# Where a load stands in the queue: moving token-major loads, rotary tables and four low parts in the preparation of a two-layer encoder

## The chip, the cores and the metric

The kernel runs on one core of a Trainium2 chip. Its engines each work off their own instruction queue in order: TensorE (PE in the profile), VectorE (DVE), ScalarE (ACT), GpSimd (POOL) and SyncE (SP), which issues nearly all transfers here. The metric is the device time of one execution in microseconds (us); lower is better. Lines are written L138 for line 138 of the kernel before; in the changed kernel the lines behind the preparation are numbered three higher (L1033 becomes L1036).

## The reference

A trunk of two layers over 1024 tokens of width 1024, with 256 memory tokens beside it. Cut to what matters here:

```python
memn = rmsnorm(mem, mem_norm_gain)
for l in range(2):
    h = rmsnorm(x, norm_gain[l])
    mk, mv = jnp.split(memn @ w_mem_kv[l], 2, axis=-1)       # memory keys and values, both layers
    if l == 0:
        qa, ka, va, qb, kb, vb, qm, gate = split_cols(h @ w_in_even[0], SPLIT_EVEN)
        qa = rope_2d(rmsnorm(qa, q_norm_a), row, col)         # 8 query heads of 64
        ka = rope_2d(rmsnorm(ka, k_norm_a), row, col)         # 2 key heads of 64
        ya = global_gqa(qa, ka, va)                           # full attention
        yb = window_gqa(qb, kb, vb, sink, rel_bias)
        ym = memory_attn(qm, mk, mv)
        x = x + (concatenate([ya, yb, ym]) * silu(gate)) @ w_out_even[0]
    else:
        ...                                                   # neighbourhood attention in place of A and B
return rmsnorm(x, final_norm_gain)
```

`rope_2d` rotates pairs of a head's elements by angles of the token's grid row and column, with cosine and sine tables. Everything is float32.

## The kernel before, in words

To keep float32 accuracy on TensorE, each operand of a matmul is split into two parts: a high part (a copy in a rounded type, `wh`, `ah`, `H`) and a low part (the value less its high part, `wl`, `al`). Each product is three matmuls: high by high, high by low, low by high.

Layer 0 cannot start before its preparation, `project_a`. In program order that is:

- the tokens' and the memory's columns are loaded (L943) and scaled by the gains; group 0 of the A weights (`a_weights`) gives keys and values for four quarters of 256 tokens (`a_unit`, L851);
- `mem_keys` for layer 0: eight units of weights of 128x512 (two per head); each unit is a load (`wload`, L138), a high part on ScalarE (`wparts`, L125), a low part (L160), and twelve matmuls (L561);
- `mem_values` for layer 0: eight more units, with matmuls at L590; its low parts alternate between VectorE and GpSimd;
- `rope_tables`: gains, cosines and sines are loaded (L764, L768), and GpSimd multiplies them to four tables (L771);
- `rstd(io["mt"], ...)`: the memory's tokens again, token by row this time (token-major, four loads of 128x512, L801), squared and summed on ScalarE (L802), for the factors `rs_m` by which memory rows are normalised after the projection;
- group 1 of the A weights, the same statistics for the tokens (`stats`), key units (`k_unit`), layer 1's memory keys;
- eight query units (`q_unit`), four with group 1 and four with group 2: each takes a projection, normalises and rotates it on ScalarE, VectorE and GpSimd (the sum `rp`, L885), transposes it on TensorE (L133), splits it into a high and a low `so` buffer (L125, L129), and stores the parts with eight DMAs (group 1, L928 and L929) or four (group 2, L931);
- `mem_values` for layer 1 behind the second unit of group 2, all of its low parts on VectorE; and at last `mem_q`, the memory queries of layer 0 (L242), from `w_e` weights.

The raw weights have four buffers, `wraw`; a load into one waits until the high and the low part that read it are made. The order on each engine is not that of the program text alone: the framework's scheduler simulates a timeline (`schedule_with_timeline_sim`) and sorts instructions by it, subject to priorities and to fences. A fence is written as `tc.issue_after(x)`: what is issued inside it does not come before `x` in the order. The lines that bear on the change:

```python
def behind(self):                                             # L120
    return self.tc.issue_after(self.loaded.ins) if self.loaded else nullcontext()
...
self.raws.append(d)                                           # L139, wload: every raw weight load in turn
...
e = self.either() if self.wsplit[1] == "both" else nc.gpsimd if self.wsplit[1] == "pool" else nc.vector
e.tensor_tensor(lf, raw, hf, op=OP.subtract)                  # L160, wparts: the low part
...
with self.behind():                                           # L800, rstd: a token-major load
    nc.sync.dma_start(t, src[b][:, j * 512:j * 512 + 512])
```

`raws[0]` to `raws[3]` are group 0 of the A weights, `raws[4]` to `raws[11]` the eight units of layer 0's memory keys. So `raws[6]` is their third unit, `raws[8]` the fifth and `raws[11]` the eighth. `either()` returns VectorE and GpSimd in turn. In front of `rope_tables` the fence `self.loaded` is the last load of the memory's columns.

## Time and profile before

| what | value |
|---|---|
| time, median of three runs | 1488.08 us (1487.84 to 1490.82) |
| profiled execution: span on the core (the page gives no other time of it) | 1486.8 us |
| median less span | 1.28 us |
| TensorE busy | 1467.6 us, 99% of the span |
| VectorE, ScalarE, GpSimd busy | 69%, 56%, 43% |
| preparation: from the start to the first scores matmul of layer 0 (L1033) | 143.63 us |
| TensorE idle from 20 to 70 us, and from 100 to 125 us | 2.74 us, 1.42 us |

Times inside the profile count from the start of the span. A row of the timeline has the start, the length, engine, line, operation, output and inputs, and in brackets how long the engine was idle before it and what ended that. A row with x4 joins four neighbours of a kind. Rows of a stretch have, after its bounds and length, the busy time and count of PE, PE's weight loads, DVE, ACT and POOL, then the granted TensorE clock, the transfers' share and GB/s. SPq marks rows of SP's queue: the issue of a transfer, not its duration.

### The profile page before, as it was taken

What the parts mean: (1) busy time and instruction counts of PE and PEld (TensorE: products, weight loads), DVE (VectorE), ACT (ScalarE), POOL (GpSimd) and SP (SyncE); (2) the same over time, 40 slices, a digit from 0 to 9 for tenths busy, and PEclk for the clock granted to TensorE, in tenths of its full rate; (3) what the DMA queues carried; (4) which work ended last, traced back from release to release, by engine and by line L of the source; (5) the groups of instructions that cost most, each with busy time, mean ns of one, the idle gap of its engine ahead of it and who ended that gap; (6) DMA issues with size and microseconds to landing.
All of it is one profiled execution on the core that took longest, in us unless ns stands there. A gap on an engine that the chain in (4) does not pass through costs nothing.

```text
span 1486.8 us, 25511 instructions
## 1 busy us (share of the span) xinstructions
PE 1467.6 (99%) x8433; PEld 1274.7 (86%) x8433; DVE 1030.7 (69%) x2124; ACT 837.2 (56%) x1877; POOL 644.2 (43%) x767
## 2 busy tenths in 40 slices
PE   9999999999999999999999999999999999999998
PEld 8898898988888788888879987888998898888886
DVE  6687777677776577776687776664446787778674
ACT  7743665556655456654544444444446777777454
POOL 1223668556765746543450000001425556665454
PEclk9999999999999999999999999999999999999999
DMA  8966334434443424388553343567665568789834
GB/s 287 306 160 181 118 125 160 123 120 133 126 137 112 155 78 144 100 276 303 187 176 127 128 135 137 157 169 241 233 242 170 188 198 269 246 283 323 314 105 144
DMA packets 173860, 271.92 MB, mean 183 GB/s; under 512 B 15648, under 2 KB 96800, under 8 KB 172704
## 3 DMA queue, kind: packets, MB, share of 16 engines
q1 hardware_dynamic: 173296, 270.20, 56.4%
q8 instruction: 67, 1.10, 0.3%
q14 instruction: 65, 0.53, 0.1%
q10 hardware_dynamic: 432, 0.09, 0.0%
HBM read 174.28 MB, written 83.89 MB: 174 GB/s over the span
## 4 chain that ended last, share of the span: by engine, by line
PE 86%; DMA 6%; DVE 3%; ACT 2%; issue 1%; SPq 1%; POOL 1%; POOLq 0%; ACTq 0%; DVEq 0%
PE pj L242 16%; PE pj L62 11%; PE x L1617 6%; PE tr L133 6%; PE pv L1066 4%; PE y L1617 4%; PE pv L62 3%; PE s L62 3%; PE pj L1332 3%; PE tr L62 3%; PE sa L1332 2%; PE pv L1617 2%; PE sa L1033 2%; PE s L1332 2%; PE sa L1034 2%; PE pj L851 2%
## 5 line engine op out<-in xcount | busy, mean ns | idle before, releaser
L542 DVE TENSOR_TENSOR pl<-tr,ph 128x512 fp32r<-128x512 f32 (+2 forms) x352 | 203.9, 594 | 45.5 <-ACT ph L125 43.6
L125 ACT ACTIVATE ph<-tr 128x512 fp32r<-128x512 f32 (+2 forms) x352 | 176.2, 522 | 103.7 <-PE tr L133 79.7
L242 PE MATMUL pj<-H,wh 128*128 128x512 f32 x704 | 233.2, 411 | 0.6 <-DVE vt L313 0.2
L158 POOL TENSOR_SCALAR wh<-wraw 128x512 fp32r<-128x512 f32 x48 | 32.2, 673 | 275.2 <-PE x L1617 236.0
L125 ACT ACTIVATE wh<-wraw 128x384 fp32r<-128x384 f32 (+1 forms) x163 | 88.7, 553 | 99.6 <-PE pj L1332 12.2
L242 PE MATMUL pj<-H,wl 128*128 128x512 f32 x352 | 139.2, 395 | 0.0
L242 PEld LDWEIGHTS pj<-H,wh 128*128 128x128 f32 x704 | 120.6, 189 | 19.3 <-issue 0.6
L62 PE MATMUL pj<-H,wh 128*128 128x512 f32 x384 | 121.0, 396 | 0.0
L1119 POOL TENSOR_SCALAR pn<-pn,st 128x384 f32<-128x384 f32 (+1 forms) x128 | 72.7, 569 | 102.1 <-DVE st L1118 62.0
L133 PE MATMUL tr<-ident,P 128*128 128x128 f32 x752 | 115.4, 273 | 0.3 <-POOL P L719 0.2
L1279 POOL TENSOR_TENSOR wl<-wraw,wh 128x384 fp32r<-128x384 f32 x56 | 62.9, 1125 | 91.5 <-ACT wh L125 89.2
L1117 ACT ACTIVATE pn<-pn,st 128x384 f32<-128x384 f32 (+1 forms) x128 | 75.1, 587 | 41.8 <-DVE st L1114 40.5
L133 PEld LDWEIGHTS tr<-ident,P 128*128 128x128 f32 x752 | 88.9, 140 | 8.2 <-POOL P L719 1.2
L1039 ACT ACTIVATE P<-sa,st 128x1024 f32<-128x1024 f32 x64 | 71.4, 1117 | 35.3 <-PE tr L133 19.1
L1041 POOL TENSOR_SCALAR P<-P,st 128x1024 f32<-128x1024 f32 x64 | 74.6, 1169 | 27.9 <-DVE st L1040 27.3
L1038 DVE TENSOR_REDUCE st<-sa 128x1 f32<-128x1024 f32 x64 | 77.5, 1218 | 8.3 <-PE sa L1034 7.6
L62 PE MATMUL s<-k,q 128*128 128x384 f32 (+1 forms) x352 | 81.2, 327 | 0.0
L242 PEld LDWEIGHTS pj<-H,wl 128*128 128x128 f32 x352 | 66.2, 188 | 15.1
L62 PE MATMUL pj<-H,wl 128*128 128x512 f32 x192 | 75.6, 394 | 0.0
L160 POOL TENSOR_TENSOR wl<-wraw,wh 128x512 fp32r<-128x512 f32 x52 | 69.6, 1341 | 10.3 <-ACT wh L125 7.8
L851 PE MATMUL pj<-ah,H 128*128 128x256 f32 x384 | 70.8, 282 | 1.0 <-ACT ah L125 0.6
L62 PEld LDWEIGHTS pj<-H,wh 128*128 128x128 f32 x384 | 66.6, 188 | 5.4
(568 smaller groups left out, 4186.7 us busy)
## 6 DMA issues: line engine op xcount, KB each, us to landing
wraw<-w_o SPq DMA_DIRECT2D x52, 256.0 KB, 3.7
y<-yb SPq DMA_DIRECT2D x24, 512.0 KB, 3.4
wraw<-s SPq DMA_DIRECT2D x64, 192.0 KB, 3.9
wraw<-w_e SPq DMA_DIRECT2D x44, 256.0 KB, 3.3
k<-k SPq DMA_DIRECT2D x42, 256.0 KB, 5.9
s<-bias SPq DMA_DIRECT2D x56, 192.0 KB, 2.0
wq<-w_o SPq DMA_DIRECT2D x40, 256.0 KB, 3.3
y<-sg SPq DMA_DIRECT2D x18, 512.0 KB, 3.5
```

Of the source, the lines that this page charges most:

```text
L62: return lambda *a, **k: self.tc.keep_in_program_order(getattr(self.engine, name)(*a, **k))
L125: return self.nc.scalar.activation(out, in_, AF.Copy, scale=scale)
L133: self.turned = self.fence = self.pe.transpose(o, i, self.ident)
L242: self.pe.matmul(a[:, :n], s[:, kt % UNIT, :], m, start=(kt == 0 and i == 0), stop=(kt == KT - 1 and i == 2))
L542: self.low = nc.vector.tensor_tensor(pl[:, :n], tr[:, :n], ph[:, :n], op=OP.subtract)
L851: self.last = nc.tensor.matmul(a[:, b * 256:(b + 1) * 256], x[kt][:, t], w, start=(kt + b + i == 0), stop=(kt == KT - 1 and i == 2), skip_ ...
L1038: nc.vector.tensor_reduce(st[:, 0:1], s, axis=AX.X, op=OP.max, negate=True)
L1041: self.normal = nc.gpsimd.tensor_scalar(pt, pt, st[:, 2:3], 0.5, op0=OP.mult, op1=OP.mult)
L1117: nc.scalar.activation(o, o, AF.Exp, bias=st[:, 0:1], scale=-1.0, accum_out=st[:, 2:3])
L1119: self.normal = normal = nc.gpsimd.tensor_scalar(o, o, st[:, 3:4], 0.5, op0=OP.mult, op1=OP.mult)
L1332: last = nc.tensor.matmul(bank, s[:, k, :], y[3 * u + k][m][:, cols], start=start and u + k + e == 0, stop=u == 1 and k + e == 4, skip_gro ...
L1617: self.last = nc.tensor.matmul(bank, ws[s][:, k, :], b[k][m], start=start and k + i == 0, stop=k == UNIT - 1 and i == 2, skip_group_check= ...
```

## The change

Two edits in `project_a`. First, the memory's token-major loads now come ahead of `rope_tables` in the program, behind a fence on the fifth unit of the memory's key weights (before: the third); the three loads of the rotary tables get the eighth unit as their fence (before: the memory's columns). This fence also holds for the loads of A weights and token statistics that follow in the text, which had the third unit's. Second, the eight low parts of layer 1's memory values alternate between VectorE and GpSimd; before all eight were on VectorE. Eight turns of `either()` leave its state as it was.

```diff
@@ -985,10 +985,11 @@
         end = [self.mem_keys(w0, mem, kvd[0], ("pj", "tr"), "so", "rt1")]
         self.wsplit = ("act", "both")
         end.append(self.mem_values(w0, mem, kvd[0], "so"))
+        vm = self.st("xv", [128, 2])
+        self.loaded = self.raws[8]
+        self.rstd(io["mt"], [0, 1], vm, self.rs_m)
+        self.loaded = self.raws[11]
         self.rope_tables()
-        vm = self.st("xv", [128, 2])
-        self.loaded = self.raws[6]
-        self.rstd(io["mt"], [0, 1], vm, self.rs_m)
         self.wsplit = ("act", "dve")
         w1 = self.a_weights(1)
         self.stats(range(4))
@@ -1009,7 +1010,9 @@
         for q in range(4):
             after(self.q_unit(self.a_unit(w2, q), q, 2, qa, qd))
             if q == 1:
+                self.wsplit = ("act", "both")
                 self.mem_values(w1m, mem, kvd[1], "so")()
+                self.wsplit = ("act", "dve")
         while late:
             flush()
         return self.mem_q(io["w_e"], E_QM)
```

The scheduler makes a new order of the preparation from it, on every engine. Behind the preparation the orders agree. Three places matter. SP's queue after the fourth unit of the memory's keys (`wraw_600` is the fifth unit, `wraw_654` the eighth, `xt<-mt` the memory's token-major loads), before:

```order
L138 DMA wraw_581<-w_mem 128x512
L764 DMA so_770<-g_kq 128x256
L768 DMA rt_135_772<-c_cos 128x512
L768 DMA rqn_778<-c_sin 128x512
L801 DMA xt_786<-mt 128x512
L801 DMA xt_789<-mt 128x512
L801 DMA xt_792<-mt 128x512
L138 DMA wraw_600<-w_mem 128x512
L138 DMA wraw_618<-w_mem 128x512
L138 DMA wraw_636<-w_mem 128x512
L801 DMA xt_795<-mt 128x512
L138 DMA wraw_654<-w_mem 128x512
```

and now:

```order
L138 DMA wraw_581<-w_mem 128x512
L138 DMA wraw_600<-w_mem 128x512
L801 DMA xt_772<-mt 128x512
L138 DMA wraw_618<-w_mem 128x512
L138 DMA wraw_636<-w_mem 128x512
L801 DMA xt_775<-mt 128x512
L138 DMA wraw_654<-w_mem 128x512
L801 DMA xt_778<-mt 128x512
L801 DMA xt_781<-mt 128x512
L764 DMA so_792<-g_kq 128x256
L768 DMA rt_142_794<-c_cos 128x512
L768 DMA rqn_800<-c_sin 128x512
```

The fifth unit moved ahead of six transfers, and the tables behind all units. The second place is SP's queue at the end of the preparation. The difference around the stores of the query units; `wraw_1824` and `wraw_1836` are the last two units of layer 1's memory values, `wraw_2039` and `wraw_2045` the two units of layer 0's memory queries, and `so_1529` stands for the third unit's high part:

```order
+L138 DMA wraw_1800<-w_mem 128x4x128
 L912 DMA k_138<-k_138 64x1024
-L138 DMA wraw_1800<-w_mem 128x4x128
 L138 DMA wraw_1812<-w_mem 128x4x128
+L138 DMA wraw_1824<-w_mem 128x4x128
 L928 DMA q_143<-so_1357 64x256
 L929 DMA qa<-so_1357 64x256
```

and, sixteen stores on:

```order
 L929 DMA qa<-so_1444 64x256
-L138 DMA wraw_1824<-w_mem 128x4x128
-L138 DMA wraw_1836<-w_mem 128x4x128
-L138 DMA wraw_2039<-w_e 128x512
-L138 DMA wraw_2045<-w_e 128x512
 L928 DMA q_143<-so_1529 64x256
 L929 DMA qa<-so_1529 64x256
```

and, sixteen more and the first unit of group 2 on:

```order
 L931 DMA qa<-so_1737 64x2x256
 L931 DMA qa<-so_1738 64x2x256
-L599 DMA kv_108<-so_1848 128x4x128
-L599 DMA kv_108<-so_1849 128x4x128
+L138 DMA wraw_1836<-w_mem 128x4x128
+L138 DMA wraw_2039<-w_e 128x512
+L138 DMA wraw_2045<-w_e 128x512
 L138 DMA wraw_2137<-w_e 128x512
```

One of the four loads that stood between the second and the third query unit's stores moved ahead of all of them, and three behind all 36. The third place is TensorE where these three are used, now (`pj_1942` is the last query unit's projection, `pj_1750` and `pj_1751` the memory values, `pj_2051` and `pj_2078` the memory queries):

```order
L851 MATMUL pj_1942<-ah_1566,H_133 128x256
L590 MATMUL pj_1750<-wh_1838,q_142 128x512
L590 MATMUL pj_1751<-wh_1838,q_142 128x512
L133 MATMUL tr_2013<-ident_63,rp_1927 128x128 x4
L242 MATMUL pj_2051<-H_118,wh_2041 128x512
L242 MATMUL pj_2051<-H_126,wh_2041 128x512
L242 MATMUL pj_2078<-H_118,wh_2041 128x512
L242 MATMUL pj_2078<-H_126,wh_2041 128x512
L590 MATMUL pj_1750<-wl_1839,q_142 128x512
L590 MATMUL pj_1750<-wh_1838,mem_177 128x512
L590 MATMUL pj_1751<-wl_1839,q_142 128x512
L590 MATMUL pj_1751<-wh_1838,mem_177 128x512
```

Before, `pj_2051<-H_118,wh_2041` came straight after the last row of `pj_1942`, and the L590 rows of `wh_1838` stood some ninety rows earlier.

## The prediction

> **What bounds the kernel now.** I read the page's busy shares first, then TensorE's waits in the preparation (everything before layer 0's first attention scores), then its stretches, and last the timeline of SP, whose queue turns out to set the end of the changed preparation.
>
> ```profile
> PE 1467.6 (99%) x8433; PEld 1274.7 (86%) x8433; DVE 1030.7 (69%) x2124; ACT 837.2 (56%) x1877; POOL 644.2 (43%) x767
> ```
>
> TensorE is busy 99% of the span and runs in order, so time can be won only where it pauses. Its waits from 0 to 110 us, and from 110 to 144 (line, what it waited for, total, times, longest):
>
> ```profile
> PE tr L133 <- POOL rp L885: 0.8, 1, 0.8
> PE tr L561 <- ACT wh L125: 0.6, 2, 0.4
> PE pj L851 <- ACT ah L125: 0.6, 1, 0.6
> PE tr L561 <- DVE wl L160: 0.5, 2, 0.2
> ...
> PE pj L590 <- ACT wh L125: 0.2, 1, 0.2
> ```
> ```profile
> PE pj L590 <- DVE wl L160: 1.3, 3, 0.8
> ```
>
> The stretches of the preparation (first column of sums PE, third DVE; then clock, DMA share, GB/s):
>
> ```profile
> 20.00:70.00 50.00, 47.26 (x339) 43.31 (x338) 29.80 (x77) 38.08 (x95) 14.59 (x12) 1.00 0.97 306
> ...
> 100.00:125.00 25.00, 23.58 (x149) 20.12 (x148) 23.01 (x53) 10.02 (x22) 5.52 (x4) 1.00 0.61 153
> 125.00:145.00 20.00, 20.00 (x121) 17.57 (x120) 11.64 (x27) 5.65 (x11) 6.00 (x6) 1.00 0.72 197
> ```
> ```profile
> 34.00:39.00 5.00, 3.90 (x26) 3.08 (x25) 2.03 (x7) 3.00 (x9) 1.29 (x2) 1.00 0.92 315
> ...
> 59.00:62.00 3.00, 1.58 (x12) 1.18 (x11) 1.80 (x5) 1.84 (x6) 1.55 (x2) 1.00 1.03 391
> ```
>
> From 20 to 70 us the transfers are the limit (DMA 0.97), from 100 to 125 VectorE is (23.01 of 25 us, TensorE 23.58), and from 125 on TensorE is full. Three pauses of before are open to the early part of the change: 1.10 us at the memory keys (5.00 less 3.90), 0.2 at L590, 1.42 at 59 to 62.
>
> **The change part by part.** *Early loads.* TensorE's pause rows, and what stood behind them:
>
> ```profile
> 35.48 0.38 PE L561 MATMUL tr<-q,wh 128*128 128x256 f32 x1 [0.37 <-ACT wh L125]
> ...
> 61.39 0.62 PE L851 MATMUL pj<-ah,H 128*128 128x256 f32 x3 [0.59 <-ACT ah L125]
> ```
> ```profile
> 34.80 0.63 ACT L125 ACTIVATE wh<-wraw 128x512 fp32r<-128x512 f32 x1 [0.78 <-DMA wraw<-w_mem]
> ```
> ```profile
> 22.81 0.43 SPq L764 DMA_DIRECT2D so<-g_kq  x1
> ...
> 24.63 2.28 SPq L801 DMA_DIRECT2D xt<-mt  x3
> 27.02 2.75 SPq L138 DMA_DIRECT2D wraw<-w_mem  x3
> ```
>
> The fifth key unit was issued at 27.02 behind six other transfers; now it is SP's next row and they follow, mixed with the later units. Its buffer comes free only with VectorE's first low parts:
>
> ```profile
> 26.30 1.96 DVE L160 TENSOR_TENSOR wl<-wraw,wh 128x512 fp32r<-128x512 f32 x3
> ```
>
> So SP now stands from 22.8 to about 27 with nothing issued, but from 27 on the key units find a shorter queue. Seven transfers are moved behind them: six of 256 KB and one of 128, 1.66 MB, 5.4 us at the 306 GB/s of the row above. The key pauses need 2 us, so I take them as gone; at worst (the dry 4 us come back later) nothing is won. The 0.8 us wait for the rotated keys (L133) goes because that transpose now stands 42 rows later, with 42 x 0.12 = 5 us more matmuls ahead of it (three matmuls end 0.62 after the first starts, one 0.38: 0.12 apart). A row's end is modelled, so each pause is 0.26 (0.38 less 0.12) longer between starts than as idle time: 1.10 + 0.2 + 1.42 = 2.7 idle, seven pauses, 2.7 + 1.8 = **4.5 us of lead** for TensorE at 62 us; bounds 0 and 4.5.
>
> The moved tables and statistics cost nothing as far as cover goes: the rotary tables are first read here,
>
> ```profile
> 58.32 0.42 DVE L880 TENSOR_TENSOR rt<-rqn,c_cosk 128x256 f32<-128x256 f32 x1
> ```
>
> and in the changed order they are issued by 35.4 (eleven rows behind 27.02, at the 0.76 of the three at 24.63), 23 us ahead of that read. The memory's row factors are read by VectorE's scaling of the projected keys, and no TensorE wait above names them. Were that cover gone, the projections' PSUM buffers would come free later and the lead would shrink by as much.
>
> *Low parts on GpSimd.* Four of eight L160 subtractions leave VectorE (0.69 us each) for GpSimd:
>
> ```profile
> L160 POOL TENSOR_TENSOR wl<-wraw,wh 128x512 fp32r<-128x512 f32 x52 | 69.6, 1341 | 10.3 <-ACT wh L125 7.8
> ```
> ```profile
> 110.76 1.28 POOL L885 TENSOR_TENSOR rp<-rt,rt 128x512 f32<-128x512 f32 x1 [2.31 <-DVE rt L882]
> ```
> ```profile
> 111.11 1.48 DVE L160 TENSOR_TENSOR wl<-wraw,wh 128x512 fp32r<-128x512 f32 x1
> 112.59 0.68 DVE L160 TENSOR_TENSOR wl<-wraw,wh 128x512 fp32r<-128x512 f32 x1
> ```
>
> GpSimd's take 1.34 us. Beside a GpSimd sum the same VectorE subtraction took 1.48 us, the next one, alone, 0.68: each GpSimd operation can hold VectorE by up to 0.8. The trace has no moved split, so its price on VectorE lies between -0.69 (nothing held) and +0.1.
>
> [...]
>
> *What decides the end: the units' stores.* Of the four moved splits three stood ahead of `so_1530`, while `wl_1827` now stands ahead of it instead of behind: two fewer, 1.4 us. Three GpSimd splits may hold VectorE by 2.4. With the lead, `so_1530` is written 4.5 + 1.4 - 2.4 = **3.5 us earlier**; bounds -1.0 (no lead, full hold) and 5.9 (all lead, no hold). I take the full hold, as VectorE's share (23.01 of 25) leaves hardly a gap in which to run beside GpSimd. This matters because of SP:
>
> ```profile
> 100.88 0.51 SPq L928 DMA_DIRECT2D q<-so  x1
> ...
> 111.62 1.17 SPq L138 DMA_DIRECT2D wraw<-w_mem  x2
> 112.89 0.92 SPq L138 DMA_DIRECT2D wraw<-w_e  x2
> 115.26 0.47 SPq L928 DMA_DIRECT2D q<-so  x1
> ...
> 126.68 2.65 SPq L931 DMA_DIRECT2D qa<-so  x4
> ```
> ```profile
> 115.26 0.69 DVE L129 TENSOR_TENSOR so<-tr,so 128x512 fp32r<-128x512 f32 x1
> ```
>
> Before, the last memory unit and the two units for layer 0's memory queries (`wraw_1836`, `wraw_2039`, `wraw_2045`) were issued at 112 to 113.8, between the second and third unit's stores. In the changed order they stand behind all 36 stores. Before, `so_1530` was written at 115.95 and the last store issued at 129.33, 13.4 later. Sixteen stores alone took 10.7 (100.88 to 111.62, 0.67 each), so fourteen and the last four need at least 9.4 + 2.65 = 12.0. I take 13.4, since the VectorE work between is the same: 115.95 - 3.5 + 13.4 = **125.8** for SP to reach the three loads (124.4 by the other end). How long they take:
>
> ```profile
> wraw<-w_mem SPq DMA_DIRECT2D x2, 256.0 KB, 3.3
> wraw<-w_e SPq DMA_DIRECT2D x2, 256.0 KB, 4.1
> ```
>
> The first `w_e` unit follows 0.6 after, lands 4.1 later and is copied in the 0.63 of ACT's row above: `wh_2041` at **131.1** (0.8 less, if it lands like `w_mem`). TensorE, 4.5 us early, would want it at about 127: a **new pause of 4 us**, released by ACT's copy behind a DMA. What follows it:
>
> ```profile
> 131.60 0.63 PE L242 MATMUL pj<-H,wh 128*128 128x512 f32 x2
> 132.07 0.39 PE L242 MATMUL pj<-H,wl 128*128 128x512 f32 x1
> ...
> 138.10 0.60 PE L133 MATMUL tr<-ident,rp 128*128 128x128 f32 x4
> 138.46 0.48 PE L242 MATMUL pj<-H,wh 128*128 128x512 f32 x1
> ...
> 143.63 0.40 PE L1033 MATMUL sa<-k,q 128*128 128x512 f32 x1
> ```
>
> Before, 12.0 us lay from the first L242 to layer 0. Now four L590 matmuls have moved behind it (4 x 0.235 = 0.9) and one group of four transposes ahead (0.4): 12.5. Layer 0 begins at 131.1 + 12.5 = **143.6**, against 143.63. From there the order on every engine is the old one. The span stays 1486.8, the median lies 1.3 above it (1488.08): **1488.1 us**. The lead is won early and given back at the stores.
>
> **The rivals.**
>
> *A, the lead is kept.* GpSimd's splits fall beside VectorE's short operations, `so_1530` comes 5 us earlier (110.95), SP needs 12.0 behind it, the load lands in 3.3: `wh_2041` at 110.95 + 12.0 + 0.6 + 3.3 + 0.63 = 127.5, layer 0 at 140.0, **1484.4**. For it: SP's pace of 0.67 and the free 0.68 rows; against it: the 1.48 row and VectorE's 23.01.
>
> *B, slower.* The place is SP's row of `wraw_1836`, the price one us per us that SP reaches it after 125.8, and it loses from there on. If VectorE writes `so_1530` no earlier than before, SP is through at 129.35, `wh_2041` is there at 134.7, layer 0 begins at 147.2: +3.6, **1491.7**. For it: VectorE is nearly full from 100 to 125, so a lead of TensorE need not reach it. Against: two subtractions less ahead of it.
>
> *C, the early pauses stay* (the change doesn't do what it says), since the 4 us in which SP issues nothing at 23 to 27 are lost in a stretch where DMA is 0.97 busy. Then `so_1530` gains only 1.4 less a hold of 0.8, 0.6: +3.0 by the same chain, **1491.1**.
>
> *D, the clock falls in the new pause.* The granted clock (third figure from the end) at the kernel's end, where TensorE has little to do:
>
> ```profile
> 1478.00:1480.00 2.00, 0.75 (x8) 0.66 (x6) 1.70 (x5) 0.99 (x4) 1.07 (x1) 1.00 0.04 14
> 1480.00:1482.00 2.00, 0.62 (x4) 0.41 (x4) 1.71 (x5) 0.38 (x1) 1.42 (x3) 0.72 1.08 382
> ```
> ```profile
> 1.31 4.21 PE L970 MATMUL pj<-rp 128*128 128x512 f32 x9 [1.31 <-POOL rp L966]
> ```
>
> It falls after some 3 us of little work, and the first nine 512-column matmuls took 4.21, 0.23 more each than at 132. Nine such after the pause cost 2 us: 145.6, **1490.1**, where the pause is over 3 us. [...]
>
> **How the numbers follow.** A measurement of this kernel tells about 0.2%, 3.0 us, from no change. Chances: forecast 0.45, A 0.22, B 0.15, C 0.08, D 0.10. Faster by over 0.2%: most of A (0.19) and 0.05 of the forecast's spread, 0.24. Slower: 0.13 of B, half of C (0.04), 0.02 of D and 0.02 of the forecast, 0.21. Within 0.2%: 0.55. The forecast's own range is 1485.9 (12.0 for SP and the short landing, -2.2) to 1490 (another 2 us of the lead held back on VectorE); the range for 8 in 10 takes in A and nearly B, 1484.3 to 1491.5.
>
> **What would show it.** Right: no pause over 0.2 us at 34 to 62; SP's first load behind the stores at 125 to 126.5; one TensorE pause of 3 to 5 us near 127, ended by ACT `wh` with a DMA behind it; L1036's first matmul (L1033 before) at 142.5 to 145; VectorE's two-input operations at 1.3 to 1.5 us beside GpSimd's L160. Wrong: no such pause (A), the loads after 128.5 (B), pauses over 1 us still at 34 to 39 (C), a clock under 1.00 behind the pause (D), or any difference after layer 0 begins.

## The result, and the profile after

The changed kernel takes 1501.87 us (median of four runs, 1499.97 to 1502.44) against 1487.96 (1486.95 to 1490.82) for the kernel before on the same chip: a ratio of 1.0092, with an interval of 1.0079 to 1.0105. By the ratio it is 13.7 us slower (the medians are 13.9 apart); the forecast was 1488.1, no change, with a range up to 1491.5. The profiled execution of the changed kernel took 1499.97 us over a span of 1498.2, against 1486.8 before: 11.4 of the 13.7 us can be read in the traces.

The page's busy line after:

```profile
PE 1470.3 (98%) x8433; PEld 1277.7 (85%) x8433; DVE 1036.5 (69%) x2120; ACT 838.0 (56%) x1877; POOL 651.7 (44%) x771
```

TensorE executes the same 8433 matmuls. It is busy 2.7 us longer, so it idles 8.7 longer. Where, is read by laying the start of the same matmul, counted from the first, side by side in both traces:

| matmul | place | start before, us | later after, us |
|---|---|---|---|
| 480 | layer 1's memory keys (L561) | 72.6 | +0.0 |
| 720 | query units, a projection (L851) | 100.9 | +0.2 |
| 780 | among the query units, transposes (L133) | 111.0 | +4.4 |
| 900 | query units, a projection (L851) | 129.8 | +2.3 |
| 971 | first scores of layer 0 (L1036) | 143.6 | +8.45 |
| 1080 | layer 0, a projection (L242) | 164.4 | +9.1 |
| 1500 | layer 0, transposes of probabilities | 231.3 | +11.7 |
| 8400 | end | 1475.5 | +11.4 |

So nearly all of it is lost before 240 us, in four places. One caution: two profiles of one and the same kernel can lie some 3 us apart at matmul 720 already, and agree better from there on (see "Chance, and a tile's place"). TensorE's waits in the changed kernel, from 0 to 110 us, from 110 to 153, and from 153 to 260 (line, what it waited for, total, times, longest):

```profile
PE pj L590 <- DVE rqn L877: 2.3, 1, 2.3
PE tr L561 <- DVE wl L160: 1.4, 2, 1.2
...
PE pj L590 <- DVE wl L160: 1.2, 1, 1.2
PE tr L133 <- DVE rs_m L783: 0.5, 1, 0.5
...
PE pj L590 <- ACT wh L125: 3.5, 1, 3.5
...
PE tr L133 <- POOL P L655: 1.3, 1, 1.3
PE sa L1036 <- DVE q L129: 0.7, 1, 0.7
```

**1. The early lead is not won.** Of the pauses for ScalarE's `wh` at L561 none is left; a second profile of the kernel before, taken later, has none of them either. But GpSimd's four table products (L771), which before ran from 30.25 to 35.3, when VectorE sat idle, now run from 37.85 to 43.8. GpSimd and VectorE in the changed kernel:

```profile
37.85 1.28 POOL L771 TENSOR_TENSOR c_cosk<-rt,so 128x512 f32<-128x512 f32 x1 [36.59 <-DMA rt<-c_cos]
39.08 1.73 POOL L771 TENSOR_TENSOR c_cosq<-rt,so 128x512 f32<-128x512 f32 x1
...
43.79 1.79 POOL L837 TENSOR_TENSOR al<-x,ah 128x512 fp32r<-128x512 f32 x1
```
```profile
38.03 1.65 DVE L160 TENSOR_TENSOR wl<-wraw,wh 128x512 fp32r<-128x512 f32 x1 [0.16 <-DMA x<-w_a]
...
42.64 1.21 DVE L783 SCALAR_TENSOR_TENSOR rs_m<-iq_t,rs_m 128x2 f32<-128x2 f32 x1
...
44.37 1.76 DVE L160 TENSOR_TENSOR wl<-wraw,wh 128x512 fp32r<-128x512 f32 x1
```

And the same stretch of the kernel before:

```profile
30.25 1.29 POOL L771 TENSOR_TENSOR c_cosk<-rt,so 128x512 f32<-128x512 f32 x1 [29.00 <-DMA rt<-c_cos]
...
35.46 0.69 DVE L160 TENSOR_TENSOR wl<-wraw,wh 128x512 fp32r<-128x512 f32 x1 [6.20 <-ACT wh L125]
```

A low part that takes 0.69 alone takes 1.65 beside a table product and 1.76 beside the subtraction L837 that GpSimd now begins right behind the tables; products of two columns take 1.05 to 1.25. TensorE waits for exactly these: 1.18 us at 39.7, 0.49 at 43.9 (`rs_m`), 1.18 at 46.2. The second profile of the changed kernel has the same stretched operations (1.63 and 1.76 us, and 1.06 to 1.25 for the small products). The stretch from 20 to 70 us shows the sum (third busy figure VectorE: 29.80 before for the same 77 instructions), beside the two later stretches that the prediction quoted of before:

```profile
20.00:70.00 50.00, 46.53 (x334) 42.57 (x334) 35.15 (x77) 38.12 (x92) 17.22 (x12) 1.00 0.87 283
100.00:125.00 25.00, 22.07 (x132) 18.93 (x131) 21.07 (x47) 8.72 (x19) 8.10 (x6) 0.93 0.52 126
125.00:145.00 20.00, 16.45 (x102) 14.61 (x101) 11.20 (x28) 4.63 (x9) 3.86 (x3) 0.91 0.62 176
```

VectorE spends 5.35 us more, and TensorE is busy 0.73 less; nothing is won by 70 us. Second profiles confirm the loss on VectorE: its first 178 operations, the same ones in both orders, take 78.2 and 79.9 us in two profiles of before, 85.3 and 85.2 in those of the changed kernel.

**2. ScalarE's queue holds the rotation.** ScalarE after, from 101 us:

```profile
101.39 0.63 ACT L125 ACTIVATE wh<-wraw 128x512 fp32r<-128x512 f32 x1 [1.54 <-DMA wraw<-w_mem]
104.51 0.63 ACT L125 ACTIVATE wh<-wraw 128x512 fp32r<-128x512 f32 x1 [2.48 <-DMA wraw<-w_mem]
105.04 0.19 ACT L779 ACTIVATE iq_t<-rss 128x8 f32<-128x8 f32 x1
...
105.62 0.58 ACT L125 ACTIVATE so<-tr 128x512 fp32r<-128x512 f32 x1
```

and before:

```profile
99.62 0.58 ACT L125 ACTIVATE so<-tr 128x512 fp32r<-128x512 f32 x1
100.70 0.63 ACT L125 ACTIVATE wh<-wraw 128x512 fp32r<-128x512 f32 x1 [0.50 <-DMA wraw<-w_mem]
101.24 0.19 ACT L779 ACTIVATE iq_t<-rss 128x8 f32<-128x8 f32 x1
...
102.61 0.63 ACT L125 ACTIVATE wh<-wraw 128x512 fp32r<-128x512 f32 x1 [0.69 <-DMA wraw<-w_mem]
```

In the new order the copies of the second and the third unit of layer 1's value weights, each waiting for its load, stand ahead of the query units' root (L779) and of the first high part to be stored. Before, the second stood ahead of the root alone and the third behind both. Root and high part come 4 to 6 us later, VectorE's rotation after them, and TensorE pauses 2.3 us for it (1.2 in the second profile); then its clock is halved for 3.4 us. Starts at 110 are 0.43 apart, where 0.23 is usual:

```profile
108.73 0.50 PE L590 MATMUL pj<-wh,q 128*128 128x512 f32 x1 [2.27 <-DVE rqn L877]
...
110.16 0.63 PE L590 MATMUL pj<-wh,mem 128*128 128x512 f32 x1
110.58 0.63 PE L590 MATMUL pj<-wl,q 128*128 128x512 f32 x1
```

The first query store goes out at 106.23 (100.88 before); `so_1530`, the third unit's low part, is done at 120.0 (116.0 before).

**3. The three loads behind the 36 stores.** SP, ScalarE, and TensorE after:

```profile
130.41 2.64 SPq L931 DMA_DIRECT2D qa<-so  x4
133.14 0.55 SPq L138 DMA_DIRECT2D wraw<-w_mem  x1
133.74 6.25 SPq L138 DMA_DIRECT2D wraw<-w_e  x6
```
```profile
136.25 0.63 ACT L125 ACTIVATE wh<-wraw 128x512 fp32r<-128x512 f32 x1 [7.15 <-DMA wraw<-w_mem]
```
```profile
136.93 1.11 PE L590 MATMUL pj<-wh,q 128*128 128x512 f32 x2 [3.55 <-ACT wh L125]
```

SP reaches them at 133.1, TensorE pauses 3.55 us, released by ScalarE's copy behind a transfer, and its clock is halved again (third figure from the end):

```profile
110.00:112.00 2.00, 2.00 (x6) 1.52 (x6) 1.93 (x5) 0.00 (x0) 1.22 (x1) 0.50 0.40 98
...
138.00:140.00 2.00, 2.00 (x9) 1.71 (x8) 1.76 (x7) 1.03 (x3) 0.24 (x1) 0.50 0.36 130
```

Between matmuls 900 and 971 this costs 6.1 us.

**4. Layer 0.** TensorE waits 0.7 us for the first `q`, and 1.3 near 235 for GpSimd's scaling of the memory probabilities (L655). GpSimd and VectorE there, after and then before:

```profile
234.14 2.80 POOL L655 TENSOR_SCALAR P<-P,st 128x256 f32<-128x256 f32 x4
...
233.68 1.56 DVE L514 TENSOR_TENSOR yb<-yb,sg 128x1024 f32<-128x1024 f32 x1
```
```profile
222.35 1.85 POOL L655 TENSOR_SCALAR P<-P,st 128x256 f32<-128x256 f32 x4
...
224.50 1.87 DVE L514 TENSOR_TENSOR yb<-yb,sg 128x1024 f32<-128x1024 f32 x1
```

The order on each engine is the same there. In this profile of before, GpSimd's four operations were through when VectorE's product began; after, VectorE began first and GpSimd's took 0.95 us longer. With a late restart it costs 2.5 us.

### The profile page after: what moved, and what is told of

The parts are those of the page before. It is cut to its first block, busy times and chain, and to the rows that moved or that the text cites. A ratio compares the mean times of both kernels' runs of the same rounds, so it can differ in the third digit from the quotient of the medians.

```text
span 1498.2 us, 25517 instructions
## 1 busy us (share of the span) xinstructions
PE 1470.3 (98%) x8433; PEld 1277.7 (85%) x8433; DVE 1036.5 (69%) x2120; ACT 838.0 (56%) x1877; POOL 651.7 (44%) x771
## 4 chain that ended last, share of the span: by engine, by line
PE 82%; DVE 6%; DMA 5%; ACT 3%; issue 2%; POOL 2%; SPq 0%; POOLq 0%; DVEq 0%; ACTq 0%
PE pj L242 15%; PE pj L62 11%; PE x L1620 6%; PE tr L133 5%; PE pv L1069 4%; PE y L1620 4%; PE pv L62 3%; PE s L62 3%; PE pj L1335 3%; PE tr L62 3%; PE sa L1335 2%; PE pv L1620 2%; PE s L1335 2%; PE sa L1036 2%; PE sa L1037 2%
## 5 line engine op out<-in xcount | busy, mean ns | idle before, releaser
L242 PE MATMUL pj<-H,wh 128*128 128x512 f32 x704 | 234.2, 413 | 0.4 <-DVE vt L313 0.2
L242 PE MATMUL pj<-H,wl 128*128 128x512 f32 x352 | 139.0, 395 | 0.0
L242 PEld LDWEIGHTS pj<-H,wh 128*128 128x128 f32 x704 | 121.1, 190 | 19.0 <-POOL wh L158 0.6
L1122 POOL TENSOR_SCALAR pn<-pn,st 128x384 f32<-128x384 f32 (+1 forms) x128 | 72.3, 566 | 105.2 <-DVE st L1121 66.1
L133 PE MATMUL tr<-ident,P 128*128 128x128 f32 x752 | 116.1, 273 | 2.0 <-POOL P L655 1.3
L133 PEld LDWEIGHTS tr<-ident,P 128*128 128x128 f32 x752 | 88.8, 140 | 10.9 <-POOL P L655 2.6
L1042 ACT ACTIVATE P<-sa,st 128x1024 f32<-128x1024 f32 x64 | 71.5, 1117 | 35.3 <-PE tr L133 17.7
L160 POOL TENSOR_TENSOR wl<-wraw,wh 128x512 fp32r<-128x512 f32 x56 | 75.7, 1355 | 15.2 <-ACT wh L125 12.6
L242 PEld LDWEIGHTS pj<-H,wl 128*128 128x128 f32 x352 | 66.2, 188 | 15.2
L851 PE MATMUL pj<-ah,H 128*128 128x256 f32 x384 | 70.7, 283 | 0.0
```

What stands on the lines that cost most here:

```text
L133: self.turned = self.fence = self.pe.transpose(o, i, self.ident)
L242: self.pe.matmul(a[:, :n], s[:, kt % UNIT, :], m, start=(kt == 0 and i == 0), stop=(kt == KT - 1 and i == 2))
L1122: self.normal = normal = nc.gpsimd.tensor_scalar(o, o, st[:, 3:4], 0.5, op0=OP.mult, op1=OP.mult)
```

## The experiments

All ratios are against the kernel before, measured beside it on the same chip. "Layer 0" is how much later its first scores begin than in the first profile of before (143.63 us), "matmul 1500" and "8400" the same for these.

| run | time, us | ratio, interval | layer 0 | 1500 | 8400 |
|---|---|---|---|---|---|
| changed kernel | 1501.87 | 1.0092 (1.0079 to 1.0105) | +8.5 | +11.7 | +11.4 |
| first edit alone | 1495.34 | 1.0046 (1.0029 to 1.0063) | +1.6 | +8.6 | +9.1 |
| second edit alone | 1494.28 | 1.0036 (1.0018 to 1.0054) | -0.6 | +5.3 | +4.6 |
| tables early | 1498.60 | 1.0063 (1.0039 to 1.0087) | +5.5 | +10.6 | +10.1 |
| three loads from ScalarE | 1495.14 | 1.0036 (1.0019 to 1.0053) | +5.0 | +7.4 | +9.9 |
| ScalarE's copies held back | 1509.59 | 1.0141 (1.0123 to 1.0158) | +5.6 | +10.0 | +21 |
| before, sink from SP | 1494.29 | 1.0035 (1.0019 to 1.0052) | -0.4 | +3.5 | +2.9 |
| second edit, sink from SP | 1499.46 | 1.0075 (1.0058 to 1.0091) | +0.2 | +8.6 | +9.5 |
| candidate 1 | 1497.80 | 1.0058 (1.0043 to 1.0073) | +2.4 | +8.4 | +9.4 |
| second edit, sink early | 1499.02 | 1.0064 (1.0043 to 1.0085) | +1.6 | +4.2 | +9.6 |
| before, sink early | 1496.59 | 1.0050 (1.0028 to 1.0073) | -2.6 | -1.7 | +5.2 |
| candidate 2 | 1496.26 | 1.0052 (1.0034 to 1.0069) | +1.7 | +1.9 | +6.8 |
| before again | 1490.30 | one time | -2.7 | -0.9 | +1.7 |
| before, 32 unused bytes | 1494.65 | 1.0042 (1.0026 to 1.0058) | -2.3 | -2.0 | +3.0 |
| before, sink early in 64 bytes | 1495.05 | 1.0053 (1.0033 to 1.0073) | +0.2 | +0.4 | +4.3 |
| candidate 2 in 64 bytes | 1496.17 | 1.0048 (1.0027 to 1.0069) | -0.1 | +1.9 | +6.9 |
| changed kernel again | 1503.19 | one time | +10.4 | +15.0 | +14.6 |
| before, 256 unused bytes | 1488.11 | 0.9997 (0.9984 to 1.0009) | -1.5 | -1.1 | +0.1 |
| candidate 2 in 256 bytes | 1492.28 | 1.0021 (1.0004 to 1.0037) | -1.3 | +0.9 | +4.3 |

**The edits apart.** The first edit alone leaves out the two `self.wsplit` lines of the second; the second alone leaves the loads and the tables as they were.

> The first edit alone (token-major loads and rotary tables later), all eight low parts of layer 1's memory values on VectorE. Theory T (three in-order queues): the four table products on GpSimd now run at 38 to 44 us beside VectorE's work and cost the early lead; ScalarE has the copy of wh_1790 ahead of the rotation's square root iq_t_1429 as in the changed kernel and waits for its load, 2 to 5 us at 100 to 113 us; but wraw_1836 and wraw_2039 stay ahead of the third unit's stores, so the pause of 3.5 us at 133 with its half clock is missing or short. 1491 to 1495 us. Rival R (GpSimd's splits hold VectorE, the second edit is the cause): 1486 to 1489 us, no pause over 1 us at 100 to 113.

> The second edit alone (half of the low parts on GpSimd), loads and tables as before. Theory T: tables early as before, ScalarE's wh_1790 behind iq_t_1429, wraw_1836 and wraw_2039 ahead of the third unit's stores (only wraw_2045 stands at the end), so within 3 us of before: 1486 to 1491 us. Rival R: the four GpSimd subtractions hold VectorE, the rotation chain and the stores are late, 1494 to 1502 us.

Both times came out above what was expected, the first by 0.3 us, the second by 3.3. Neither edit alone delays layer 0's start by more than 1.6 us, and in both the last pause (L590 for ScalarE's `wh`, 3.5 us) is absent: with the first edit alone one of the three loads goes behind the stores, with the second alone one too, while the other two are issued at 110 to 116, between them. Only the two together put all three there. The second edit alone costs the preparation nothing that can be told (-0.6; from matmul 720 to 971 it takes 42.7 us, as before), so four low parts on GpSimd are not the trouble at their own place.

What each run does lose comes at the start of layer 0. ScalarE and VectorE with the second edit alone:

```profile
149.92 0.34 ACTq L1916 DMA_DIRECT2D sink<-sink_b  x1
150.30 1.12 ACT L1041 ACTIVATE P<-sa,st 128x1024 f32<-128x1024 f32 x1 [3.16 <-DMA wraw<-w_e]
```
```profile
154.63 0.17 DVE L1917 TENSOR_SCALAR sink<-sink 128x8 f32<-128x8 f32 x1 [2.92 <-DMA sink<-sink_b]
154.71 0.68 DVE L313 TENSOR_TENSOR vt<-pj,rows 128x512 f32<-128x512 f32 x1
```

The load of the window attention's sink vector, issued by ScalarE, waits for a weight transfer to land, and holds the second exponential back 3.16 us. The sink lands at 154.6 (150.2 before), and VectorE's negation of it stands ahead of the next eviction, `vt`, for which TensorE then waits 1.6 us. In the kernel before and in the changed one ScalarE issues this load ahead of the first exponential, where the wait (2.3 and 1.9 us) holds up no TensorE row. With either edit alone the scheduler has put it behind the first exponential. So a single edit is not half of the change: each makes an order of its own at the start of layer 0 too, and its total is not a share of the change's. Tables early and three loads, below, have this order as well.

**The three traced causes, undone one by one.** Tables early: `rope_tables` back to its old place, with its old fence. Three loads: raw weights 41 to 43 issued by ScalarE. Copies held: `wh_1778` and `wh_1790` fenced behind the high parts of the first query units, so that ScalarE cannot stand at their loads (the diffs show the lines that matter).

```diff
+        self.rope_tables()
         vm = self.st("xv", [128, 2])
         self.loaded = self.raws[8]
         self.rstd(io["mt"], [0, 1], vm, self.rs_m)
         self.loaded = self.raws[11]
-        self.rope_tables()
```
```diff
-            d = self.nc.sync.dma_start(raw, src)
+            q = self.nc.scalar if len(self.raws) in (41, 42, 43) else self.nc.sync
+            d = q.dma_start(raw, src)
```
```diff
-            self.copy(hf, raw)
+            with self.tc.issue_after(self.highs[1 if len(self.raws) == 38 else 0].ins) if len(self.raws) in (37, 38) else nullcontext():
+                self.copy(hf, raw)
```

> Both edits, but the rotary tables keep their early fence (the memory's columns) and their place ahead of the token-major loads; SP still has the three last loads behind all 36 stores. Theory T: GpSimd's table products run at 30 to 36 us while VectorE is idle, the lead of 3 to 4 us at 60 us is there; iq_t_1429 stands ahead of wh_1790; the pause behind the stores stays, 3 to 6 us near 128 with half clock. 1489 to 1495 us. Rival R (the splits) or a rival in which only the place of the three loads counts: 1499 to 1503 us.

> Both edits as changed; the three last loads (wraw_1836, wraw_2039, wraw_2045) are issued from ScalarE's queue instead of SP's, where they no longer stand behind the 36 stores. Theory T: the pause of 3.5 us at 133 and the half clock behind it are gone, the pause at 106 to 113 stays: 5 to 7 us faster than the changed kernel, 1494 to 1498 us. Rival R (the place of the loads does not matter since VectorE is the limit): within 2 us of the changed kernel, 1500 to 1503 us.

> Both edits as changed; only the copies of the second and third unit of layer 1's memory values (wh_1778, wh_1790) are held behind the query units' so copies in ScalarE's queue, so that the rotation's square root iq_t_1429 no longer stands behind a copy that waits for a load. Theory T (a late load blocks ScalarE's queue): TensorE's pause of 2.3 us at 106 and the half clock at 110 to 113 are gone, matmul 780 (of all, by order) is within 1.5 us of before instead of 4.4 late, so_1530 written at 114 to 117 instead of 120. The pause at the end stays or grows, since all last loads still stand behind the stores: 1496 to 1502 us. Rival (VectorE, held by GpSimd's subtractions, is late by itself): the pause at 106 stays over 1.5 us and so_1530 stays at 119 to 121.

Of the three times only that of the three loads lay where it was expected; tables early came 3.6 us above, the copies held back 7.6. In the traces each removes most of its own loss and leaves the others. With the tables early TensorE is 1.55 us ahead at matmul 720 instead of 0.2 behind. That is less than two profiles of one kernel differ there, and so shows no lead. What follows is lost at the next two places (TensorE's waits of that run):

```profile
PE pj L590 <- DVE rqn L877: 1.7, 1, 1.7
...
PE sa L1036 <- DVE q L129: 3.0, 1, 3.0
PE pj L590 <- ACT wh L125: 2.9, 1, 2.9
```

With the three loads on ScalarE's queue nothing is lost between matmuls 900 and 971 (-0.1 against +6.1). With the copies held, matmul 780 is 0.85 late against 4.4, and `so_1530` is done at 117.8 instead of 120.0; the pause at the end stays, 2.3 us. That run's total cannot be compared, since its fences also changed the order in layer 1, where it lost another 11 us.

**The sink load.** It stood in the way in both single edits, so it was moved: to SP's queue in the kernel before and with the second edit alone, and in a candidate with all the mended causes (tables early, three loads on ScalarE).

```diff
-        nc.scalar.dma_start(sink, self.io["sink_b"].to_broadcast([128, 8]))
+        nc.sync.dma_start(sink, self.io["sink_b"].to_broadcast([128, 8]))
```

> The kernel before with one transfer moved: the sink's load of layer 0 is issued by SP instead of ScalarE. A control for the next two runs. Theory T: before, ScalarE's queue waits for this issue too (2.3 us, ahead of the exponential's table), but TensorE is full there: within 2 us of the kernel before, 1486 to 1491 us. Rival: the wait costs TensorE time before as well: faster by 2 us or more.

> The second edit alone, and the sink's load issued by SP. With the second edit alone preparation ended 0.6 us earlier than before, but layer 0 lost 3.3 us by 164 us: ScalarE's issue of the sink's load, now between the first two exponentials, waited until a weight load with the same semaphore had landed. Theory T: that loss goes, 2 to 4 us faster than the second edit alone: 1489 to 1492 us, and no TensorE wait on vt (L313) over 0.5 us at 150 to 157. Rival (the loss is VectorE's or GpSimd's lateness): the same wait stays and the time is 1493 to 1496 us.

> Token-major loads behind the fifth unit, tables early as before, low parts half on GpSimd, the three last loads issued by ScalarE, the sink's load by SP: each of the suspected costs taken away at once. Theory T: the lead of 1.5 us is kept to the end of preparation, which ends at 141.5 to 143.5 us; 1484 to 1489 us, level with the kernel before or a little better. Rival (the splits on GpSimd cost by themselves, or the loads moved to ScalarE hold its queue): preparation ends after 145 us, 1491 us or more.

None of the three gained anything; all lie above their expected times. On SP the sink stands behind weights and lands later still (154.6 us in the kernel before, where it was 150.2, and 156.9 with the second edit alone, where it was 154.6); VectorE waits for it in the kernel before too, and TensorE 1.5 to 3.9 us for `vt` behind it (VectorE in the kernel before with the sink on SP):

```profile
154.59 0.17 DVE L1915 TENSOR_SCALAR sink<-sink 128x8 f32<-128x8 f32 x1 [5.67 <-DMA sink<-sink_b]
```

Then both the load and the negation were moved into the preparation, into a tile of 32 bytes in the pool that lives through the program:

```diff
+        self.sink = self.st("sink", [128, 8], pool=self.base)
+        nc.sync.dma_start(self.sink, io["sink_b"].to_broadcast([128, 8]))
```

> The second edit alone; the sink's load and its negation on VectorE are done at the start of preparation instead of at the start of layer 0. In the runs before, VectorE's negation stood ahead of vt (L313) in its queue and waited for that load until 154.6 us (second edit alone) or 156.9 (load issued by SP). Theory T: the wait goes, TensorE's wait for vt at 150 to 157 is under 0.5 us, layer 0 loses less than 1 us by 170 us, and the time is 2 to 5 us below the second edit alone (1494.3): 1489 to 1492 us. Rival (VectorE or GpSimd is late anyway): the wait stays, 1493 to 1496 us.

> The kernel before with the same: the sink's load and negation at the start. Theory T: before, the load lands in time (VectorE waited 0.5 us there), so nothing is won: within 2 us of before, 1487 to 1491 us. Rival (any new order of the preparation costs 3 to 6 us, since before's is a lucky one): 1492 to 1497 us.

> Token-major loads behind the fifth unit, tables early as before, half of the low parts on GpSimd, the three last loads issued by ScalarE, the sink at the start. Preparation ended 2.4 us late in the candidate before it, and layer 0 lost 6 us at the sink. Theory T: those 6 us go: 1490 to 1494 us, preparation ending at 144 to 147. Rival: another wait takes their place, 1495 us or more.

The waits for `vt` went, as expected, but the times did not fall. The kernel before with the sink early stood 1.7 us ahead at matmul 1500 and 5.2 behind at 8400, though TensorE idled only 1.4 us more in between than in the first profile of before. So a loss without a pause had come in, and the spread of one and the same kernel was unknown.

**Chance, and a tile's place.** The two kernels again; the kernel before with an unused tile of 32 bytes in that pool and nothing else; and the sink tile padded to 64 bytes:

```diff
+        self.pad = self.st("pad", [128, 8], pool=self.base)
```

> The kernel before once more, for a second profiled execution of the same instructions: how much of what the other profiles show behind the preparation is chance. Theory T: the preparation ends within 0.5 us of 143.6, and TensorE's wait for GpSimd's scaled P at 235 us, which several profiles have and the first of before has not, may be there: up to 2.5 us. Rival: both are as in the first profile, and the 235 us wait belongs to the change.

> The kernel before with one unused tile of 32 bytes per partition in the base pool and nothing else; the instructions and their order stay. It asks why the kernels with the early sink load lost time slowly along layers 0 and 1 without a pause: there each 512-column matmul of L242 that reads H began 234 ns after the one ahead (median) against 232 in the kernel before, and the sink tile in the base pool had moved H from address 42496 to 42528 of its partition. Theory (place in memory: H no longer begins at a multiple of 64 bytes): 234 ns here too, 4 to 5 us over the 8433 matmuls, 1492 to 1494 us. Rival (the early load or the missing wait does it): 232 ns and 1489 to 1490.

> The kernel before with the sink load and negation at the start, as in the earlier run of that kind, the tile padded to 64 bytes, so that H begins at 42560, again a multiple of 64. Theory (place in memory): L242's matmuls return to 232 ns, and the slow loss of some 4 us that run had behind 300 us goes: 1490 to 1492 us against 1496.6. Rival (the early load does it, or any move of H): 234 ns and 1495 to 1497.

> Both edits of the change, but the tables in their old place ahead of the statistics, the last three loads from ScalarE's queue, and the sink load and negation at the start in a tile of 64 bytes. Theory (place in memory): the earlier run of this kernel with 32 bytes stood 1.6 us behind at the end of the preparation and lost some 4 more along the layers; without those it stands at +1 to +3, 1490 to 1493 us. Rival: as before, 1496.

> The changed kernel once more. What is the change's own should come back: layer 0's first attention scores 7 to 10 us later than in the kernel before, with the pause before the last units released by ScalarE's copy, and the tables beside VectorE's low parts. What is chance should not: the 1.3 us wait for GpSimd's L655 near 235 us may be absent. If the loss at the end of the preparation is under 4 us, the account of the three loads behind the stores falls.

The same kernel before reached layer 0 2.7 us earlier than in its first profile, more than expected, and the changed kernel 2 later: a difference below some 3 us between two starts in the table tells nothing. Nearly all of that spread arises before matmul 720. The first profile's pauses at 34 to 39 and 59 to 62 us, on which the forecast built its lead, are mostly absent from the second, in which TensorE is busy 48.77 us of 20 to 70 instead of 47.26:

```profile
20.00:70.00 50.00, 48.77 (x359) 45.54 (x358) 33.43 (x80) 39.62 (x98) 14.79 (x12) 1.00 1.00 323
```

Times between the starts of two matmuls of the same profile tell more (us; two values are two profiles):

| kernel | 100 to 720 | 720 to 971 | 971 to 1500 | 1500 to 8400 |
|---|---|---|---|---|
| before | 83.4, 80.8 | 42.7, 43.1 | 87.7, 89.5 | 1244.1, 1246.7 |
| before, 256 unused bytes | 82.6 | 42.5 | 88.1 | 1245.3 |
| changed | 84.2, 85.1 | 50.9, 50.8 | 90.9, 92.3 | 1243.8, 1243.7 |
| tables early | 82.0 | 49.7 | 92.8 | 1243.6 |
| three loads from ScalarE | 85.7 | 45.4 | 90.1 | 1246.6 |
| ScalarE's copies held back | 84.4 | 47.4 | 92.1 | 1255.1 |
| candidate 2 in 256 bytes | 82.3 | 43.0 | 89.9 | 1247.6 |

From 720 to 971 the change costs 8 us in both profiles, and the candidates, with the tables early and the three loads on ScalarE, take 43.0 to 44.4 us there. The early loads gain nothing that can be told: the five profiles with both edits and the tables early take 82.0 to 83.9 from 100 to 720, much like the kernel before. The five with the tables late take 84.2 to 85.7, though two with the early order of before reach 84.9 and 85.0.

The wait for L655 appeared in one of the two profiles of before (0.9) and in both of the changed kernel. The changed kernel's own loss is confirmed: 8.5 and 10.4 us at layer 0's start. The pause before the last units is the same; the one for VectorE's rotation is half as long (TensorE's waits from 110 to 153 in the second profile):

```profile
PE pj L590 <- ACT wh L125: 3.6, 1, 3.6
PE pj L590 <- DVE rqn L877: 1.2, 1, 1.2
PE pj L590 <- DVE wl L160: 1.0, 1, 1.0
```

The unused tile alone costs 0.42%, with the order on every engine the same. It moves the tiles of the pools that are laid out behind it, among them `H`, the tokens' columns that L242 and other matmuls read, from address 42496 in its partition to 42528 in the built program. L242's matmuls in the kernel before, and with the 32 bytes (in the rows, duration in ns: least, median, most):

```profile
L242 PE MATMUL pj<-H,wh x500: 385/393/497, 299.6 to 647.5; 128*128 128x512 f32 x167
```
```profile
L242 PE MATMUL pj<-H,wh x498: 388/397/505, 299.8 to 647.2; 128*128 128x512 f32 x166
```

From start to start of neighbouring L242 matmuls the median is 234 ns instead of 232. Part of the theory fell: at 42560, again a multiple of 64, it was still 234 ns, and the time stayed at 1.0053. So a last pair of runs put `H` at 42752, a multiple of 256, by a tile of 256 bytes.

> The kernel before with an unused tile of 256 bytes per partition in place of the one of 32: H begins at 42752 (a multiple of 256; before it was 42496, also one; 42528 and 42560, where L242's matmuls took 234 and 233 to 234 ns, are none). Theory (H, or what stands behind it, has to begin at a multiple of more than 64 bytes): 232 ns again, 1488 to 1490 us. Rival (the address of before is good for another reason, or any moved address costs): 233 to 234 ns and 1493 to 1495 us.

> Both edits, the tables in their old place, the last three loads from ScalarE's queue, the sink load and negation at the start, its tile now 256 bytes long. With the 64 byte tile the slow loss along the layers was still there and the time 1496.2 us. Theory (H at a multiple of more than 64 bytes): 232 ns in L242 and 1490 to 1493 us, level with the kernel before or a little behind it. Rival (any moved address costs): 1495 to 1497 us.

With 256 unused bytes the kernel before is itself again (0.9997, 232 ns, median row 393):

```profile
L242 PE MATMUL pj<-H,wh x498: 385/393/507, 300.6 to 647.8; 128*128 128x512 f32 x166
```

In all profiles the median follows the place: 232 ns in the twelve with `H` at 42496 and the two at 42752, 234 in the two at 42560, 234 or 235 in the four at 42528. From matmul 1500 to 8400 the six with 234 or 235 took 1248.1 to 1251.0 us; the others took 1243.5 to 1247.6, but for the copies held back. So the losses without a pause of the early sink came from the place of tiles, `H` or others moved with it, and the verdicts on those kernels have some 0.4% in them that the sink has no part in. The candidate (both edits, tables early, three loads on ScalarE, sink early, `H` well placed) is the best form of the change that was run: 1.0021, slower than before by 0.6 to 5.5 us, and 0.71% (10.6 us) better than the change as it was made. No kernel that was run beats the kernel before.

## Why the prediction was wrong, point by point

- **The key pauses go: not shown.** None of L561's waits for ScalarE's `wh` is left between 34 and 39 us in the first profile. But the second profile of the kernel before has none of them, nor the pause at 61 us, and the second of the changed kernel has one of 0.2.
- **"4.5 us of lead": the step that failed first.** The term was read from the pauses of a single execution. From 20 to 70 us TensorE idled 2.74 us in it and 1.23 in the second of the same kernel, so much of the lead was chance. No kernel with the early loads shows any of it, those with the tables early included.
- **"The moved tables and statistics cost nothing as far as cover goes": wrong.** The cover that was checked was the readers', 23 us away. What runs beside GpSimd's table products was not asked. They had run in VectorE's idle 6.2 us; moved 7.6 us, they and the subtraction behind them ran beside its low parts, stretched these to 1.65 and 1.76, and TensorE waited 2.9 us in three pauses. These three waits came back in the second profile. Lead at 70 us: 0, the lower bound given.
- **"`so_1530` 3.5 us earlier; bounds -1.0 and 5.9": measured 4.0 later.** This is the term that set the result. Of the 7.6 us between forecast (112.4) and measurement (120.0), 4.5 are the lead that wasn't there. The prediction also left out ScalarE: it followed VectorE, SP and TensorE in the new order, and not the engine in whose queue a copy had moved ahead of L779 and two ahead of the first high part. Holding those copies back brought `so_1530` to 117.8, 2.2 us earlier, by one profile of each kernel.
- **The low parts on GpSimd: right in kind.** Beside the moved subtractions at 95.3, 105.2 and 115.6 us VectorE's operations took 1.1, 0.9 and 1.1 us longer than alone, 3.0 where the sum had 2.4. Two of the three were products of eight columns, just below the 1.3 to 1.5 us forecast:

```profile
105.51 1.02 DVE L781 TENSOR_TENSOR iq_t<-iq_y 128x8 f32<-128x8 f32 x1
...
116.11 1.25 DVE L871 SCALAR_TENSOR_TENSOR rss<-rss,e 128x8 f32<-128x8 f32 x1
```

  The second edit alone left layer 0's start where it was.
- **The chain behind `so_1530`: right.** Fed with the measured 120.0 us it gives 120.0 + 13.4 = 133.4 for SP at the three loads (measured 133.14), + 5.3 = 138.7 for `wh_2041` (its copy ended at 138.2), + 12.5 = 151.2 for layer 0 (152.08). It holds for two more kernels with these loads behind the stores: 149.3 from the tables early (149.1 measured) and 149.0 from the copies held back (149.2). The pause was 3.55 us, near the forecast's 4, ended by ScalarE's copy behind a transfer, and taking the loads out of SP's queue removed it. It ended with the copy of the last memory unit, one unit ahead of `wh_2041`, which the forecast had named.
- **Rival B was the case, beyond its stated price.** Its rate, one us per us that SP comes later than 125.8, gives 143.6 + 7.3 = 150.9. Its condition was set at "no earlier than before"; 4 us later than before was not thought of. What rival C supposed, that no lead comes, held too, but not by the pauses that it named.
- **Rival D came on top.** The clock fell behind the 3.55 us pause and also behind the 2.27 one, each time for 3.4 us; the busy sum grew 2.7 us. In the second profile it fell at the first of these pauses, 3.6 us there, for 6.8 us. Its chance of 0.10 rested on an estimate of the author that no run shows: each of the two pauses of that length that were traced, 3.55 and 3.6 us, had a fall.
- **"Behind layer 0's start nothing differs": wrong.** The order is the same, but from matmul 971 to 1500 the changed kernel takes 90.9 and 92.3 us, the kernel before 87.7 and 89.5. Which part belongs to the later arrival and which to chance stays open: the L655 wait comes up in either kernel.
- **The time.** Of 13.7 us, 10.6 go with the tables, the three loads and the sink mended together. The remaining 3.1 (interval of that ratio 0.6 to 5.5) were not taken apart.

## What to carry to other kernels

Before moving an operation of GpSimd, look at what VectorE does where it comes from and where it goes; that its readers come later is only half the cover (here low parts of 0.69 us took 1.65 and 1.76 beside GpSimd's operations). For every engine that the new order touches, ScalarE's queue included, look for an instruction that waits on a transfer and has moved ahead of the path that sets the end; a queue in order passes the wait on (here a root and a high part came 4 to 6 us later). Take two profiles of the same kernel before building a forecast on pauses of a few us in all. And compare buffers' addresses before blaming a wait that is not there (32 unused bytes cost 0.42% here).

## What the runs showed of the hardware that was not expected

- **With tiles moved, matmuls were slower.** With `H` at 42528 or 42560 instead of 42496 or 42752, the 512-column matmuls of L242 started 234 or 235 ns apart instead of 232, and the kernel before took 0.4% longer with the 32 unused bytes. Of the four addresses the two multiples of 256 gave 232 ns, those 32 and 64 past one did not; 128 was not tried, nor which of the moved tiles counts beside `H`.
- **The clock fell after short pauses, but not each time.** In the first profile of the changed kernel it halved for 3.41 us after pauses of 2.27 and 3.55 us. Near 238 us the second profile of the changed kernel shows it halved after TensorE had waited 1.00 us for L655 (with four transposes spread over 1.7 us behind), and the first keeps 1.00 after 1.28 us at the same place:

```profile
236.00:238.00 2.00, 0.87 (x4) 0.28 (x2) 1.04 (x2) 0.00 (x0) 2.00 (x3) 1.00 0.17 53
...
240.00:242.00 2.00, 2.00 (x6) 1.61 (x5) 1.70 (x2) 0.27 (x1) 1.92 (x3) 0.50 0.03 9
```

  The half-clock stretches lasted 3.41 us, and once 6.83 (from 136.68 in the second profile). Two of the pauses here were shorter than that, 1.00 and 2.27 us, and in the 3.41 us before these falls TensorE's rows were busy 2.03 and 1.14 us, so a stretch that was only partly idle sufficed. Two falls lie 27.31 us apart in the first profile (109.78 and 137.09), 8 times 3.413, and two 102.40 in the second (136.68 and 239.08), 30 times. No run here shows what sets these distances, nor why the clock fell once and not the other time at the same place.
- **An issue of a transfer held its engine.** With the second edit alone ScalarE stood 3.16 us at the issue of the 4 KB sink, with an exponential queued behind it, until another weight's transfer had landed. The wait is one of the program: the framework has the issue wait for the semaphore on which that weight's landing is counted too. In the kernel before the last part of that landing was counted at 146.67 us, and the issue began at 146.69.
